# An encoder block on one core: at the projection's end, two form parts go to raw weight buffers, the last pair of rows is spread over the first units, and group 2's weight rows go behind it

## The chip, the cores and the metric

The kernel runs on one core of one Trainium2 chip. The metric is the device time of one execution in microseconds: before the change 1247.73 us, the median of three runs (1246.71 to 1248.21). Smaller is better.

## What is computed

One layer of a bidirectional encoder on 1024 tokens of width 1024, in float32:

```
u = RMSNorm(x);  [q|k|v|cB|cC|cH|gA|gB] = u @ W_in
y_A = neighbourhood_attention(q, k, v) @ W_A
y_B = (cB * conv3(cC * cH)) @ W_B
m = sigmoid(gA) * y_A + sigmoid(gB) * y_B
x = x + m @ W_o
x = x + relu(RMSNorm(x) @ W1)^2 @ W2
```

The change lies where `x + m @ W_o` (the projection, here) ends and `RMSNorm(x) @ W1` (the MLP's first product) begins.

## The kernel before

**Precision.** Every float32 operand is scaled and split into two float16 parts, a high and a low one; a product is three matmul passes (high x high, high x low, low x high). The high part is made by ACT, the low part by DVE.

**Seven products.** The MLP's first product is done by blocks with seven products instead of eight. The activations are therefore needed in seven *forms* (sums and differences of the four quarters of the rows; `sums` makes them with four additions), and the weights of each of 16 *groups* q in seven forms too. `U2[0]` (tile u2T) holds forms 0 to 3 of the activations, `U2[1]` (tile u2x) forms 4 to 6, each with high and low part and with 512 token positions.

**Pairs.** Rows are handled in four pairs: pair n holds blocks n and n + 4 of 128 tokens. For each pair `normal` scales the two blocks of x (ACT), `form_sums` makes the forms in one buffer (`fv[0]`, tile form; DVE), `high(n, part)` writes the high parts to a second buffer (`fv[1]`, tile v16; ACT, line 1193), and `low(n, part)` the low parts (DVE, line 1199), and then issues the transposing DMA (SP, line 1200) that puts the part in its place in `U2`. Part 0 is forms 0 to 3, part 1 forms 4 to 6. There is one form buffer and one v16 buffer, so a pair's high part waits for the transposes of the pair before.

**The order at the projection's end is written out by hand** (lines 1375 to 1404). `tail(b, half, ...)` issues one projection product of 24 matmuls (`proj`), and after it the listed operations. `sq` is a square with row sums (ACT), `row3` and `row_scale` the scale of a row (DVE, with one square root on ACT), `g1` one step of `forms_m`, which builds the seven weight forms of group 1 in spare places (one of them the tile `two` from the pool of raw weight buffers), and `tk` one step of the background list. The last pair, blocks 3 and 7, is a generator, `last_pair`, which is advanced by the units that follow.

**Units.** `unit` issues the matmuls of one product, then the evacuation of the product before (`late`), then so many `step`s of the foreground list `fg` and `tick`s of the background list `bg`. All engines work through their instructions in the order of issue. Groups 0 and 1 are each computed in two halves of 256 tokens, `quad(0, 0, 256)`, `quad(1, 0, 256)`, `quad(0, 256, 512)`, `quad(1, 256, 512)`, seven units each, with 3 steps and 5 ticks to a unit: these are the 28 half products of the text. The later groups run whole, seven units of 512 tokens. A product's result lies in one of eight PSUM banks, in three classes (d, s, o), taken in turn; it comes free with its evacuation: ACT's copy of product 1 (line 1457), DVE's `post6`, `post5`, `post2` (lines 1440, 1445, 1459), `post7` (lines 1448 to 1450), which frees three, and `post3` (1453).

**After a group.** `h_done(q)` squares the result on ACT (lines 1414, 1416), makes its seven forms with four additions on POOL (line 1159, called with `G`), and stores them to `hs` (line 1420). The result tile `as` has two buffers, so group q + 2 waits for the store of group q.

**The weights' chain** (background): `sums1(q)` scales the rows of the two raw parts (ACT, line 952), squares them for a bound (ACT, line 961) and adds forms (POOL, line 966); six half products later one column goes to a DVE cast (line 933), and two half products later a matmul with ones sums it over the partitions (`all_sum`, line 179). `prep1(q)` then takes the power of two from it (DVE, lines 182 to 412) and splits the forms (ACT line 981, DVE line 977), and goes on with `sums1(q + 1)`.

**Raw buffers.** The pool `rawp` has five buffers for raw weight parts of 512 KB. `load_upto` issues loads (SP, line 210) up to a count; `done` counts the parts that have been split, `held` the buffers lent to something else, `limit` the last part that may be loaded.

Of the kernel before, what the change touches and what calls it, by code (L numbers as in the profile page):

```python
# [10 lines left out]
F32 = mybir.dt.float32  # L11
F16 = mybir.dt.float16
BF16 = mybir.dt.bfloat16
I32 = mybir.dt.int32
AF = mybir.ActivationFunctionType
OP = mybir.AluOpType
# [36 lines left out]
def encoder_block(ctx: ExitStack, tc: tile.TileContext, x, weights, cols, gqk, rel, masks, out):  # L53
    nc = tc.nc
    V, A, G, T, SP = nc.vector, nc.scalar, nc.gpsimd, nc.tensor, nc.sync

    base = ctx.enter_context(tc.tile_pool(name="base", bufs=1))
    rawp = ctx.enter_context(tc.tile_pool(name="rawp", bufs=5))
# [38 lines left out]
    def at(c, i, n=1):  # L97
        return slice(c.start + i, c.start + i + n)
# [18 lines left out]
    fg, bg = [], []  # L117
# [88 lines left out]
    loads, loaded, done, vhome, held, limit = [], [0], [0], [], [0], [10 ** 6]  # L206
# [5 lines left out]
    def load_upto(n):  # L212
        while loaded[0] < min(n - held[0], limit[0], len(loads)):
            ch, p = loads[loaded[0]]
            loaded[0] += 1
            t = rawp.tile([128, 1024], F32, name="raw")
            load_into(t[:, :ch.widths[p][0] * ch.widths[p][1]], ch, p)
            ch.raw.append(t)
# [104 lines left out]
    g1, g2, gm2 = at(consts, 0, 8), at(consts, 20, 8), keep()  # L323
    rows = {"A": lambda j: rowsA, "B": lambda j: rowsB, "O": lambda j: rowsM}
    chunks, offset = {}, 0
    for (kind, j), pieces in plan():
# [4 lines left out]
        for p, (k, w) in enumerate(ch.widths):  # L331
            ch.offs.append(offset)
            if kind != "X" and (kind, j) != ("1", 0) and (kind, j, p) != ("1", 1, 1):
# [3 lines left out]
    cV, cConv, cA, cB, cO, c1, c2, c2x = ([chunks[k, j] for j in range(n)] for k, n in  # L337
                                              (("V", 2), ("C", 4), ("A", 4), ("B", 4), ("O", 2),
                                               ("1", 16), ("2", 4), ("X", 4)))
# [120 lines left out]
    sq = w1p.tile([128, D], F32, name="sq", bufs=1)  # L460
# [84 lines left out]
    for p in range(11):  # L545
# [7 lines left out]
        for q in (p,) if p < 6 else (2 * p - 6, 2 * p - 5):  # L553
            c = q // 2 + 3
# [306 lines left out]
    for k in range(N + 15):  # L861
        p, w = k // 16, k % 16
# [215 lines left out]
    for n in range(8):  # L1078
# [19 lines left out]
        else:  # L1098
            push(cO[0])
            tick(4)  # L1100
            y = w3p.tile([128, 4, 512], F32, name="gsum", bufs=1)
# [47 lines left out]
    U2 = (u2T,  # L1149
          w4p.tile([128, 3, 2, 4, 512], F16, name="u2x", bufs=1))  # L1150
# [4 lines left out]
    def sums(f, sub):  # L1155

        z = [f[:, i] for i in range(7)]
        for o, a, b, op in ((5, 0, 2, OP.subtract), (2, 2, 3, OP.subtract), (4, 2, 0, OP.subtract), (6, 1, 4, OP.add)):
            sub.tensor_tensor(z[o], z[a], z[b], op=op)  # L1159
            yield  # L1160

    pair_done, fv, ssq = [0], [], keep(10)
# [7 lines left out]
    def row_scale(col, n=1):  # L1170
        y = tmp(n)
        for _ in rstd(at(ssq, col, n), D, y, 9):
            pass
        return y

    def normal(b, y):
        A.activation(fv[0][:, 2 * (b // 4):2 * (b // 4) + 2].rearrange("p a t -> p (a t)"), X1[:, b], AF.Copy,
                     scale=sc[:, y])
# [9 lines left out]

    PART = ((0, 4), (4, 7))

    def high(n, part):
        a, b = PART[part]
        A.activation(fv[1][:, a:b, 0], fv[0][:, a:b], AF.Copy)

    def low(n, part):

        f, v = fv
        a, b = PART[part]
        V.tensor_tensor(v[:, a:b, 1], f[:, a:b], v[:, a:b, 0], op=OP.subtract)  # L1199
        SP.dma_start_transpose(U2[a // 4][:, :, :, :, 128 * n:128 * n + 128]  # L1200
                               .rearrange("p f s k t -> p (f s k) t"), v[:, a:b].rearrange("p f s k -> p (f s k)"))
        pair_done[0] = n + part

    def form_sums():
# [22 lines left out]
    def sums1(q):  # L1227

        ch = c1[q]
        if q == 2:  # L1230
            yield from rows_scaled(ch, g2)
        if q == 0:
            tsum[0] = U2[1][:, 2].rearrange("p s k t -> p (s k t)").bitcast(F32).rearrange("p (i c) -> p i c", i=4)
        elif q % 2 == 0:
            while q == 2 and pair_done[0] < 4:
                yield
            t = wsp.tile([128, 2, 4, 512], F32, name="tsum", tag="ws")
            for i in range(2):
                tsum[q + i] = t[:, i]
        if q != 2:  # L1240
            yield from rows_scaled(ch, g2)
        yield from forms_sum(ch, tsum[q], 3 if q else 0)

    def prep1(q):

        ch = c1[q]
        s, ch.inv = yield from scale_of(ch.sum, 9, 1)
        yield from gate(q)
        pool, tag = TAGS[q % 3]
        P = P1[q] = pool.tile([128, 7 if q else 8, 2, 512], F16, name="w16_1", tag=tag)  # L1250
        yield from forms_split(ch, tsum[q], s, P)
        ready.add(q)
        if 1 < q < 15:
            yield from sums1(q + 1)
# [1 line left out]
    SQJ = U2[1][:, 0, :, :, 384:512].rearrange("p s k t -> p (s k) t").bitcast(BF16)  # L1256
    scaled = []

    limit[0] = c1[3].first + 1

    def prep_m():

# [14 lines left out]
    def forms_m():  # L1277

        (w11, w12), (w21, w22) = ([c1[1].raw[i].rearrange("p (n m) -> p n m", n=2)[:, j] for j in range(2)]
                                  for i in range(2))  # L1280
        s = scaled[0]
        two = rawp.tile([128, 1024], F32, name="raw").bitcast(F16).rearrange("p (f i c) -> p f i c", f=2, i=2)
        held[0], limit[0] = 1, 10 ** 6
        t2 = w4p.tile([128, 2, 512], F16, name="t2", bufs=1)
        t4 = w4p.tile([128, 2, 512], F16, name="t4", bufs=1)
        k4 = lambda v: v.rearrange("p (k c) -> p k c", k=4)
        flat = {0: lambda i: P1[0][:, 7, i], 1: lambda i: two[:, 0, i], 2: lambda i: two[:, 1, i],
                5: lambda i: t2[:, i], 6: lambda i: t4[:, i]}

        def place(f, i):  # L1290
            return k4(flat[f](i)) if f in flat else M[0][:, 4 * (f - 3):4 * (f - 3) + 4, 512 * i:512 * i + 128]

        P1[1] = lambda f, i, k: place(f, i)[:, k]
        src = {0: w11, 1: w21, 2: w22, 3: w11, 4: w12, 5: w22, 6: w21}

        def hi(f):
            A.activation(place(f, 0), k4(src[f]), AF.Copy, scale=sc[:, s])

        def lo(f):
            V.scalar_tensor_tensor(place(f, 1), k4(src[f]), sc[:, s], place(f, 0), op0=OP.mult, op1=OP.subtract)  # L1300

        def add(o, a, b):
            V.tensor_tensor(o, a, b, op=OP.add)

        hi(0), hi(2), hi(1), lo(0), add(w11, w11, w12), lo(2)
        yield
        add(w12, w12, w22)
        yield
        add(w22, w22, w11), lo(1), hi(5), add(w21, w21, w22), hi(6)
        yield  # L1310
        lo(5), lo(6)
        yield
        hi(3), hi(4), lo(3)
        yield
        lo(4)
        done[0] += 1
        load_upto(done[0] + 5)
        ready.add(1)

# [15 lines left out]
    def wait(n):  # L1335
        for _ in range(n):
            yield
# [7 lines left out]
    two = []  # L1345
# [9 lines left out]
    def tail(b, half, *acts):  # L1355
        proj(b, half, acts)
        for a in acts:
            a()
# [3 lines left out]
    def sq(b, half=None):  # L1362
        if half is None:
            return lambda: square(b, 2 * (b % 4) + b // 4)
        return lambda: square(b, (6 if half == 0 else 8) + b // 4, slice(512 * half, 512 * half + 512))

    def row3(b):
        V.tensor_tensor(sc[:, at(ssq, 6 + b // 4)], sc[:, at(ssq, 6 + b // 4)], sc[:, at(ssq, 8 + b // 4)], op=OP.add)
        return row_scale(6 + b // 4)

    def do(f, *a):
        return lambda: f(*a)

    g1, tk = do(advance, chain), do(tick)
# [6 lines left out]
    tail(5, 1, sq(1), form_sums, do(high, 0, 0), g1)  # L1381
    tail(2, 1, do(high, 0, 1), sq(5), do(low, 0, 0), do(begin, 1), do(low, 0, 1))
    tail(6, 1, sq(2), form_sums, do(high, 1, 0))
    tail(3, 0, sq(6), do(high, 1, 1), do(low, 1, 0), do(begin, 2), do(low, 1, 1))
    tail(7, 0, sq(3, 0), form_sums, do(high, 2, 0), g1)
    bg.append(sums1(2))
    tail(3, 1, sq(7, 0), do(low, 2, 0), do(high, 2, 1), do(low, 2, 1), g1, tk)
    side[0] = False
    bg.extend(prep1(q) for q in range(2, 16))
    tail(7, 1, sq(3, 1), lambda: normal(3, row3(3)), tk)  # L1390
    fv[1] = wsp.tile([128, 7, 2, 512], F16, name="v16", tag="ws")

    def last_pair():
        sq(7, 1)()
        y = row3(7)
        yield from wait(3)
        normal(7, y)
        yield from wait(6)
        form_sums()
        high(3, 0), high(3, 1)  # L1400
        yield from wait(6)
        low(3, 0), low(3, 1)

    fg.append(last_pair())
    pe_done[0] = 0
# [6 lines left out]
    def h_done(q):  # L1412
        f = AS.pop(q)
        A.activation(f[:, 0:4], f[:, 0:4], AF.Relu)  # L1414
        yield
        A.activation(f[:, 0:4], f[:, 0:4], AF.Square, scale=sc[:, c1[q].inv],  # L1416
                     accum_out=sc[:, at(bsum[q // 4], q % 4)])
        yield
        yield from sums(f, G)
        SP.dma_start(HS[q // 4][:, :, q % 4], f)  # L1420
        live.remove(q)
        if q % 4 == 3:
            m = tmp()
            V.tensor_reduce(sc[:, m], sc[:, bsum[q // 4]], axis=AX, op=OP.max)
            yield
            yield from pow2(m, 14, *R[q // 4])
            r_ready[q // 4] = True
# [293 lines left out]
```

## Time and profile before

| | |
|---|---|
| Median of three runs | 1247.73 us |
| The profiled execution's own time | 1246.2 us |
| Its span, first to last instruction | 1244.4 us |
| Mean granted TensorE clock | 0.995 |
| PE busy | 1199.2 us, 96% |
| DVE busy | 926.9 us, 74% |
| ACT busy | 765.3 us, 61% |
| POOL busy | 437.0 us, 35% |

PE is TensorE's matmuls, DVE is VectorE, ACT ScalarE, POOL GpSimd, and SP the queue that issues DMAs. Times in the views are microseconds from the first instruction. A line of a timeline is: start, length, engine, line of the kernel, operation, out<-in by tile names, shape, count of merged instructions, and in brackets how long the engine stood idle before it and what ended that. A line of the waits is: who waited <- for whom, total, times, longest. A line of the windows gives for each stretch the busy time of PE, PE's weight loads, DVE, ACT and POOL, each with its count of instructions, then the granted clock of PE, the share and the rate of the DMAs. A line of the DMA issues ends with the time from issue to landing. The projection ends and the MLP begins at 646 us.

### The profile page before, as it was taken

The page shows a single profiled execution, that of the slowest core. Times are in us where ns is not written, and L with a number is a line of the kernel's source. Part 1 is how long each engine was busy: PE and PEld are TensorE (multiplying, and loading weights), DVE is VectorE, ACT ScalarE, POOL GpSimd, SP SyncE. Part 2 cuts the span into 40 slices and gives each one's busy share as a digit, 9 for nine tenths or more (in the row PEclk, how much of TensorE's full clock was granted, in tenths as well). Part 3 has the DMA queues.
Part 4 walks back from the last instruction along what each step waited for, and adds up shares of the span by engine and source line. Part 5 has one row for each costly group of instructions (what it writes and reads, how often), then busy time and mean ns, then how long its engine had stood idle before and what let it go on. Part 6 is the DMA issues. An engine that isn't in the chain of part 4 may idle for free. (4 is left out here: it accounts for less than half of the span.)

```text
span 1244.4 us, 17059 instructions
## 1 busy us (share of the span) xinstructions
PE 1199.2 (96%) x6294; PEld 575.2 (46%) x6294; DVE 926.9 (74%) x1733; ACT 765.3 (61%) x1177; POOL 437.0 (35%) x297
## 2 busy tenths in 40 slices
PE   4989999999999999999997899999999999999998
PEld 3534444444444444444456444444444444444444
DVE  6668777988557686887877655554546989999997
ACT  5777577787464454536666877877865763645430
POOL 2440003111331111101002756556557463373562
PEclk8999999999999999999998999999999999999999
DMA  6458456665651211216185454543575754436202
GB/s 256 105 191 179 82 121 135 136 120 114 135 144 40 68 51 51 68 35 253 55 164 122 157 177 149 186 151 134 182 273 175 273 192 139 170 111 241 102 34 102
DMA packets 170803, 173.35 MB, mean 139 GB/s; under 512 B 131424, under 2 KB 131936, under 8 KB 166624
## 3 DMA queue, kind: packets, MB, share of 16 engines
q1 hardware_dynamic: 170720, 172.27, 47.4%
q8 instruction: 49, 0.80, 0.3%
q14 instruction: 34, 0.28, 0.1%
HBM read 102.51 MB, written 37.75 MB: 113 GB/s over the span
## 5 line engine op out<-in xcount | busy, mean ns | idle before, releaser
L188 PEld LDWEIGHTS <-ops 128*128 128x128 f16 x1356 | 132.4, 98 | 159.4 <-issue 2.6
L188 PEld LDWEIGHTS <-w 128*128 128x128 f16 x1368 | 132.8, 98 | 142.9 <-issue 3.6
L859 PE MATMUL ps_d<-uT,w_ws 128*128 128x512 f16 x528 | 125.4, 379 | 0.0
L188 PE MATMUL ps_d<-ops 128*128 128x512 f16 (+1 forms) x528 | 118.3, 374 | 0.0
L188 PE MATMUL ps_s<-ops 128*128 128x512 f16 x492 | 113.2, 379 | 1.5 <-DVE ops L1554 1.1
L1545 ACT ACTIVATE ops<-hf,sc 128x2048 f16<-128x2048 f32 x26 | 52.0, 1999 | 95.5 <-PE ps_o L188 34.8
L1159 POOL TENSOR_TENSOR as<-as 128x512 f32<-128x512 f32 x64 | 88.0, 1376 | 40.6 <-ACT as L1416 36.9
L188 PEld LDWEIGHTS <-uT 128*128 128x128 f16 x648 | 64.5, 100 | 70.1 <-issue 5.3
L966 POOL TENSOR_TENSOR tsum<-raw 128x512 f32<-128x512 f32 x28 | 46.2, 1666 | 137.1 <-ACT raw L952 137.1
L188 PEld LDWEIGHTS <-w_s 128*128 128x128 f16 x588 | 56.8, 98 | 69.4 <-DVE w_s L977 1.9
L188 PE MATMUL ps_d<-u2x,w 128*128 128x512 f16 (+1 forms) x360 | 80.0, 372 | 0.0
L1547 DVE SCALAR_TENSOR_TENSOR ops<-hf,sc,ops 128x2048 f16<-128x2048 f32 x26 | 74.1, 2849 | 5.2 <-ACT ops L1545 5.2
L188 PE MATMUL ps_o<-ops 128*128 128x512 f16 x336 | 77.1, 379 | 0.0
L859 PEld LDWEIGHTS <-w_ws 128*128 128x128 f16 x528 | 50.8, 98 | 52.5
L188 PE MATMUL ps_o<-u2T,w 128*128 128x512 f16 (+1 forms) x324 | 71.7, 371 | 0.0
L952 ACT ACTIVATE raw<-raw,sc 128x256 f32<-128x256 f32 x172 | 70.9, 493 | 0.0
L966 POOL TENSOR_TENSOR gsum<-raw 128x512 f32<-128x512 f32 x14 | 19.0, 1376 | 131.6 <-issue 57.1
L981 ACT ACTIVATE w<-raw,sc 128x512 f16<-128x512 f32 (+1 forms) x28 | 24.6, 927 | 52.9 <-DVE sc L411 52.9
L1440 DVE TENSOR_TENSOR as<-ps_d,as 128x512 f32<-128x512 f32 (+1 forms) x15 | 10.1, 674 | 63.1 <-ACT as L1457 63.1
L806 ACT ACTIVATE sz<-sz,sc 128x384 f32<-128x384 f32 (+1 forms) x64 | 37.3, 582 | 26.5 <-DVE sc L810 13.2
L188 PE MATMUL ps_s<-u2T,w 128*128 128x512 f16 (+1 forms) x252 | 52.7, 359 | 0.0
L278 DVE SCALAR_TENSOR_TENSOR w_ws<-raw,sc,w_ws 128x512 f16<-128x512 f32 (+2 forms) x72 | 46.1, 691 | 2.4 <-ACT w_ws L291 2.4
(333 smaller groups left out, 2611.6 us busy)
## 6 DMA issues: line engine op xcount, KB each, us to landing
raw<-in_weights SPq DMA_DIRECT2D x89, 512.0 KB, 5.3
hs<-as SPq DMA_DIRECT2D x16, 1792.0 KB, 8.7
hf<-hs SPq DMA_DIRECT2D x26, 1024.0 KB, 6.3
w2x<-in_weights SPq DMA_DIRECT2D x16, 512.0 KB, 8.3
raw<-in_weights SPq DMA_DIRECT2D x16, 384.0 KB, 4.0
xt<-in_x SPq DMA_DIRECT2D x8, 512.0 KB, 10.0
gs<-s SPq DMA_DIRECT2D x4, 1024.0 KB, 6.8
x<-in_x SPq DMA_DIRECT2D x8, 512.0 KB, 9.9
```

The source lines that it names most:

```text
L188: T.matmul(ps, l, r, start=a, stop=b)
L278: V.scalar_tensor_tensor(lo, self.raw[p][:, o:o + m], sc[:, c:c + 1], hi, op0=OP.mult, op1=OP.subtract)
L806: A.activation(z, z, AF.Exp, scale=-1.0, bias=sc[:, d["mx"]], accum_out=sc[:, d["sm"]])
L859: T.matmul(ps, l, r, start=a, stop=b)
L952: A.activation(v, v, AF.Copy, scale=sc[:, at(g, 4 * i + k)])
L966: G.tensor_tensor(t[:, o], a, b, op=OP.add)
L981: A.activation(o(0), w, AF.Copy, scale=sc[:, s])
L1159: sub.tensor_tensor(z[o], z[a], z[b], op=op)
L1440: V.tensor_tensor(z[5], ps[6], z[4], op=OP.add)
L1545: A.activation(P[:, 1, 0], hf, AF.Copy, scale=sc[:, Rs])
L1547: V.scalar_tensor_tensor(P[:, 1, 1], hf, sc[:, Rs], P[:, 1, 0], op0=OP.mult, op1=OP.subtract)
```

## The change

Three things are done.

1. **Raw buffers as form buffers.** `forms_m` takes three raw buffers instead of one. Two of them (`spare`) hold the high and low parts of pair 1's part 0 and pair 2's part 1, each as pieces of at most two forms; each piece has its own ACT and DVE instruction and its own transposing DMA. Because the buffers are lent out, only one part of group 2's raw weights is loaded before; the other follows at the end of `forms_m`, and group 3's two parts at the end of `last_pair`.
2. **The last pair is spread out.** `normal(7)` is issued at once, the form sums and high parts three steps later, `low(3, 0)` six steps later, then, after three steps, the background list gets the weights' chain of group 2 (`sums1(2)`, before this in the tails) and of all later groups, and six steps later follow `low(3, 1)` and the loads. `sums1(2)` no longer waits for the last pair. In the tails the order changes too: `low(1, 0)` and the row scale come ahead of `high(1, 1)`, the steps of `forms_m` go one tail later and in one part more.
3. **The forms of groups 0 and 1** are added on DVE instead of POOL.

```diff
+    spare = []
+    def pieces(n, part):
+        a, b = PART[part]
+        if (n, part) not in ((1, 0), (2, 1)):
+            return [(a, b, fv[1][:, a:b])]
+        return [(c, min(c + 2, b), spare[i][:, :min(2, b - c)]) for i, c in enumerate(range(a, b, 2))]
     def high(n, part):
-        a, b = PART[part]
-        A.activation(fv[1][:, a:b, 0], fv[0][:, a:b], AF.Copy)
+        for a, b, v in pieces(n, part):
+            A.activation(v[:, :, 0], fv[0][:, a:b], AF.Copy)
     def low(n, part):
-        f, v = fv
-        a, b = PART[part]
-        V.tensor_tensor(v[:, a:b, 1], f[:, a:b], v[:, a:b, 0], op=OP.subtract)
-        SP.dma_start_transpose(U2[a // 4][:, :, :, :, 128 * n:128 * n + 128]
-                               .rearrange("p f s k t -> p (f s k) t"), v[:, a:b].rearrange("p f s k -> p (f s k)"))
+        for a, b, v in pieces(n, part):
+            V.tensor_tensor(v[:, :, 1], fv[0][:, a:b], v[:, :, 0], op=OP.subtract)
+            SP.dma_start_transpose(U2[a // 4][:, a % 4:a % 4 + b - a, :, :, 128 * n:128 * n + 128]
+                                   .rearrange("p f s k t -> p (f s k) t"), v.rearrange("p f s k -> p (f s k)"))
...
         elif q % 2 == 0:
-            while q == 2 and pair_done[0] < 4:
-                yield
...
-    limit[0] = c1[3].first + 1
+    limit[0] = c1[2].first
...
-        two = rawp.tile([128, 1024], F32, name="raw").bitcast(F16).rearrange("p (f i c) -> p f i c", f=2, i=2)
-        held[0], limit[0] = 1, 10 ** 6
+        three = [rawp.tile([128, 1024], F32, name="raw").bitcast(F16).rearrange("p (f i c) -> p f i c", f=2, i=2)
+                 for _ in range(3)]
+        spare.extend(three[:2])
+        two = three[2]
+        held[0], limit[0] = 3, c1[2].first + 1
+        load_upto(done[0] + 5)
...
-        hi(3), hi(4), lo(3)
+        hi(3), hi(4)
+        yield
+        lo(3)
         yield
         lo(4)
         done[0] += 1
+        held[0], limit[0] = 1, c1[3].first
         load_upto(done[0] + 5)
...
-    tail(3, 0, sq(6), do(high, 1, 1), do(low, 1, 0), do(begin, 2), do(low, 1, 1))
-    tail(7, 0, sq(3, 0), form_sums, do(high, 2, 0), g1)
-    bg.append(sums1(2))
-    tail(3, 1, sq(7, 0), do(low, 2, 0), do(high, 2, 1), do(low, 2, 1), g1, tk)
+    y = []
+    tail(3, 0, sq(6), do(low, 1, 0), lambda: y.append(row_scale(4, 2)), do(high, 1, 1),
+         lambda: (normal(2, at(y[0], 0)), normal(6, at(y[0], 1))), do(low, 1, 1))
+    tail(7, 0, sq(3, 0), form_sums, do(high, 2, 0), do(high, 2, 1))
+    tail(3, 1, sq(7, 0), do(low, 2, 0), g1, do(low, 2, 1))
     side[0] = False
-    bg.extend(prep1(q) for q in range(2, 16))
-    tail(7, 1, sq(3, 1), lambda: normal(3, row3(3)), tk)
+    tail(7, 1, sq(3, 1), g1, lambda: normal(3, row3(3)), g1)
...
         sq(7, 1)()
-        y = row3(7)
+        normal(7, row3(7))
         yield from wait(3)
-        normal(7, y)
-        yield from wait(6)
         form_sums()
         high(3, 0), high(3, 1)
         yield from wait(6)
-        low(3, 0), low(3, 1)
+        low(3, 0)
+        yield from wait(3)
+        bg.append(sums1(2))
+        bg.extend(prep1(q) for q in range(2, 16))
+        yield from wait(6)
+        low(3, 1)
+        limit[0] = 10 ** 6
+        load_upto(done[0] + 5)
...
-        yield from sums(f, G)
+        yield from sums(f, G if q > 1 else V)
```

## The prediction

> **What bounds the kernel now.** I read the waits of PE first, over the projection's end and the first half of the MLP (600 to 760 us), because PE is the engine that hardly rests, and only a wait of PE can be saved. There are two:
>
> ```profile
> PE ps_s L188 <- DVE as L1448: 6.3, 1, 6.3
> PE ps_s L179 <- DVE ones L933: 3.3, 1, 3.3
> ```
>
> Next the timeline of PE shows where they lie and what they cost.
>
> ```profile
> 646.12 1.47 PE L188 MATMUL ps_s<-u2T,w 128*128 128x256 f16 x12
> 647.43 1.47 PE L188 MATMUL ps_d<-u2x,w 128*128 128x256 f16 x12
> ...
> 665.67 2.71 PE L188 MATMUL ps_s<-u2T,t 128*128 128x256 f16 x12 [6.29 <-DVE as L1448]
> ...
> 668.18 1.64 PE L188 MATMUL ps_o<-u2T,raw 128*128 128x256 f16 x12
> ...
> 669.66 1.47 PE L188 MATMUL ps_d<-u2x,mH 128*128 128x256 f16 x12
> ...
> 704.49 0.16 PE L179 MATMUL ps_s<-ones 128*128 128x1 bf16 x1 [3.29 <-DVE ones L933]
> ```
>
> Groups 0 and 1 are computed as 28 half products of 12 matmuls, the first at 646.12, one each 1.31 us (647.43 - 646.12); a whole product of the later groups takes twice that. Half product 11 waits 6.29 us. After it two half products start 2.51 and 1.48 us apart instead of 1.31, which is 1.37 us more. The windows of 1 us say why (the number before the DMA share is the granted clock):
>
> ```profile
> 661.00:662.00 1.00, 0.00 (x0) 0.00 (x0) 0.75 (x2) 1.00 (x2) 0.00 (x0) 0.85 0.00 0
> ...
> 668.00:669.00 1.00, 1.00 (x8) 0.81 (x7) 0.00 (x0) 0.00 (x0) 0.00 (x0) 0.74 1.16 217
> ...
> 702.00:703.00 1.00, 0.00 (x0) 0.00 (x0) 0.00 (x0) 0.82 (x3) 0.24 (x1) 1.00 1.04 373
> ```
>
> The clock fell at 661.7, some 2.3 us after PE stopped, and came back at 668.5; the second wait of 3.29 us left it at 1.00. So the first wait costs 6.29 + 1.37 = 7.66 us, the second 3.29: 10.95 us are to be had, no more.
>
> The first wait's reason is on DVE, which has the last pair's work ahead of L1448, the operation that frees a bank:
>
> ```profile
> 651.23 0.74 DVE L1328 SCALAR_TENSOR_TENSOR x<-ps_d,sc,x 128x512 f32<-128x512 f32 x1
> ...
> 655.49 0.15 DVE L391 TENSOR_SCALAR sc<-sc 128x1 f32<-128x1 f32 x1
> ...
> 657.87 2.87 DVE L1159 TENSOR_TENSOR form<-form 128x512 f32<-128x512 f32 x4 [0.24 <-ACT form L1177]
> ...
> 661.33 3.96 DVE L1199 TENSOR_TENSOR v<-form,v 128x2048 f16<-128x2048 f32 x2 [0.25 <-ACT v L1193]
> 665.20 0.42 DVE L1448 TENSOR_TENSOR as<-ps_s,as 128x256 f32<-128x256 f32 x1
> ```
>
> The second wait is for group 4's all-sum (L933), which stands on DVE behind L1440, and that behind ACT's copy, which needs the store of group 0 landed, issued 8.9 us earlier. But ACT had been idle for only 0.18 us by then, so the store isn't the only late one.
>
> ```profile
> 693.89 0.61 SPq L1420 DMA_DIRECT2D hs<-as  x1
> ...
> 702.86 0.60 ACT L1457 ACTIVATE as<-ps_o 128x512 f32<-128x512 f32 x1 [0.18 <-DMA hs<-as]
> ...
> 704.28 0.16 DVE L933 CAST ones<-sc 128x1 bf16<-128x1 f32 x1
> ```
>
> **First part of the change: the last pair spread out.** normal(7) is now issued in half product 1, the form sums in 2, the first low part in 4, the second in 7, behind the bank-freeing operations of group 0 (post7) instead of ahead of them. These ACT rows complete the chain:
>
> ```profile
> 654.00 0.61 ACT L1167 ACTIVATE u2x<-x 128x512 bf16<-128x512 f32 x1
> ...
> 656.69 1.15 ACT L1177 ACTIVATE form<-x,sc 128x1024 f32<-128x1024 f32 x1 [0.54 <-DVE sc L400]
> ...
> 659.38 3.28 ACT L1193 ACTIVATE v<-form 128x2048 f16<-128x2048 f32 x2 [1.54 <-DVE form L1159]
> ```
>
> The last projection result is there at about 646.3. DVE adds it (0.74), ACT squares (0.8 with the accumulator), DVE adds the two half sums (0.2), scale to normal is 1.2 (655.49 to 656.69), normal 1.15: 650.4. Form sums 2.87: 653.3; high(3,0), 1.85, can begin at the third sum: 654.5; low(3,0), 2.2: 656.8; one bank operation, 0.4, then L1448, done by 657.6. Half product 11 wants it at 646.12 + 10 x 1.31 = 659.2. It has 1.6 us to spare, so the wait goes, and with it the slow clock: -7.66. From both sides: 0 spare if every link of this chain were 15% longer; a gain beyond 7.66 isn't possible there.
>
> What is late next?
>
> ```profile
> u2T<-v SPq DMA_TRANSPOSE x1, 6.9
> ...
> u2T<-v SPq DMA_TRANSPOSE x1, 8.5
> ```
>
> low(3,0)'s transposes go out at 656.8. Those of pairs 0 and 1 landed in 6.9 us, the last pair's in 8.5, so here 663.7 to 665.3, for half product 15 at 664.5: at worst a wait of 0.8 us, which a later wait would swallow. low(3,1) runs 658.1 to 659.9 on DVE, its transposes 661.5, and half product 19 (669.7) is the first to read them.
>
> **Second part: raw buffers.** high(1,0) no longer waits for the transposes of pair 0, at the price of smaller instructions.
>
> ```profile
> 620.54 4.72 SPq L1200 DMA_TRANSPOSE u2T<-v  x1
> ...
> 625.36 3.76 SPq L1200 DMA_TRANSPOSE u2x<-v  x1
> ```
>
> Four forms hold SP's queue for 4.72 us, three for 3.76: 0.96 a form and 0.9 for each issue. Two parts become four, so SP gets two issues more, 1.8 us; ACT and DVE get two instructions more each, about 0.2 us apiece. PE's 10 projection products cover that, and the first halves of groups 0 and 1 read only pairs 0 and 1, issued by 635 and landed within 7 us. I count nothing; without that cover it would be 2 us. The buffers are paid for by weights: the second part of group 2's rows is now loaded behind the transposes of pair 2, and both parts of group 3's behind those of pair 3.
>
> ```profile
> 649.84 3.98 SPq L1200 DMA_TRANSPOSE u2x<-v  x1
> 653.92 0.53 SPq L210 DMA_DIRECT2D raw<-in_weights  x1
> ```
> ```profile
> raw<-in_weights SPq DMA_DIRECT2D x1, 512.0 KB, 3.9
> ...
> hs<-as SPq DMA_DIRECT2D x1, 1792.0 KB, 8.9
> raw<-in_weights SPq DMA_DIRECT2D x2, 512.0 KB, 9.6
> ```
>
> 3.9 us is the landing of the load at 653.92, which also went out right behind a transpose; 9.6 that of two loads right behind the store of group 0. Nothing but the transposes is ahead here, so I take 3.9: group 2's part goes out at 650.5, lands at 654.4, and ACT reaches it at 657.5. Group 3's go out at 665.3 and land at 669.2 and 670.5 or so, while ACT comes to them at 669.3. There is nothing to spare: at 9.6 everything behind moves by 5.4 us.
>
> **Third part: the weights' chain and the sums.** Group 2's four adds are issued in half product 5 (before: 6), so its all-sum matmul stands behind half product 13 (before: 14), at 646.12 + 13 x 1.31 = 663.15. Before, DVE's first operation on its result came at 672.82 (below). From there ACT is the longest queue:
>
> ```profile
> 674.10 1.75 ACT L981 ACTIVATE w<-raw,sc 128x512 f16<-128x512 f32 x2
> ...
> 677.83 3.29 ACT L952 ACTIVATE raw<-raw,sc 128x256 f32<-128x256 f32 x8
> 681.03 1.04 ACT L961 ACTIVATE tsum<-raw 128x1024 f32<-128x1024 f32 x1
> ...
> 683.25 1.89 ACT L1414 ACTIVATE as<-as 128x2048 f32<-128x2048 f32 x1
> 685.18 2.00 ACT L1416 ACTIVATE as<-as,sc 128x2048 f32<-128x2048 f32 x1
> ```
>
> Split 3.73, rows scaled 3.20, squares 2.22, relu and square 4.02 (start to start, the last to 687.27): 13.2 us a group. DVE's six small operations between all-sum and split take 0.95:
>
> ```profile
> 672.82 0.15 DVE L182 TENSOR_SCALAR sc<-ps_o 128x1 f32<-128x1 f32 x1
> ...
> 673.64 0.14 DVE L412 TENSOR_SCALAR sc<-sc 128x1 int32<-128x1 int32 x1
> ```
>
> The sums of groups 0 and 1 go from POOL to DVE:
>
> ```profile
> 687.35 6.52 POOL L1159 TENSOR_TENSOR as<-as 128x512 f32<-128x512 f32 x4 [1.23 <-ACT as L1416]
> ```
>
> On DVE four take 2.87 (L1159 above) instead of 6.52, and group 0's store leaves 3.65 us sooner after the square. But DVE's order is fixed: behind these sums stand group 1's bank operations and the scale of group 3's weights, and for group 1 two of the sums and L1440 stand ahead of L933 of group 4.
>
> Laid end to end: post7 of group 1 and the six operations end at 665.2; ACT 3.73 and one copy 0.36: 669.3, group 3's rows landed; 3.20 + 2.22 + 4.02 : 678.8; DVE sums 2.87, a bank operation 0.34, six operations 0.95: 683.0; ACT 13.2: 696.2; DVE two sums 1.4, L1440 0.7, a third sum 0.7, L932 and L933 0.4: 699.4. Before it was 704.44, so group 4's all-sum comes **5.1 us sooner**, not 10.95. Two of these steps are bounded from both sides: sums at 6.5 like POOL's instead of 2.87 would add 3.6 and 2; a DVE that waits for nobody would take off 1. POOL's adds of group 4 lie at 689 to 695, between DVE's splits (684 to 689) and its sums, so I charge no slowing of one by the other.
>
> PE runs ahead of that: 28 half products end at 682.8. The third product of group 2 wants a bank that group 1's post7 frees; that stands behind group 3's split on DVE and comes at about 689.8, against 688.0: a wait of 1.8. The fourth ends at 695.0, and PE waits to 699.4: 4.4 us. This second wait is longer than the one before, and longer than the one that left the clock alone. The clock fell after 2.3 idle us at 661.7, so I expect it to fall again, and charge the same 1.37; the ends are 0 (as at 702) and 3.4 (half of a slow stretch of 6.8 us, all of it busy).
>
> In the Trainium skill, "TensorE: Matmul & The Clock Gate", section "What's actually happening", the clock falls after a whole idle window of about 3.4 us on a grid that runs freely. By that rule a wait of 4.4 us falls surely on a whole window in only about 3 of 10 positions, and the sum would be 5.1 without the 1.37. The 2.3 us of the trace speak against taking it literally.
>
> **Sum.** -5.1 + 1.4 = -3.7 us.
>
> ```profile
> PE ps_s L188 <- DVE ops L1554: 1.1, 2, 0.8
> ```
>
> This is the largest wait of PE behind 704, two of at most 0.8 us, and group 2's later work stands to PE as before, so I count nothing given back. The profiled execution, 1246.2 us with a span of 1244.4, would become 1242.5 (span 1240.7). The median of the runs before lies 1.5 us above it, 1247.73, so I forecast **1244.0**.
>
> **Rivals.**
> - *The clock stays full* in the new wait: -5.1, 1242.6. For it: 3.29 us left it alone. Chance 0.16.
> - *Both waits close*, PE then runs through: -10.95, 1236.8. It needs ACT's two rounds of 13.2 us to shrink by 6; only shorter DVE work speaks for it. 0.06.
> - *Taken back*: ACT's chain loses 2 to 4 us more (sums beside POOL, a late transpose), so that the all-sum comes at 701.5 to 704 and the clock falls too: -1.6 to +1, about 1247.5. 0.21.
> - *Slower*: the loads of group 3 land as the 9.6 row says. ACT, in order, stands before the row scaling until 674.9; L933 of group 3 follows at 674.9 + 3.2 + 2.2 + 0.5 = 680.8, where PE, behind half product 24, stands from 677.6; group 4's all-sum comes at 699.4 + 5.5 = 704.9, and two or three of the waits bring the clock down, 1.4 each: 704.9 + 2.8 to 4.2 against 704.4, so +3.3 to +4.7, about 1251.7. It costs more than the change gains from a landing of some 7.5 us on. 0.13.
> - *Forecast*: 0.44, from 1241.5 to 1246.
>
> About 0.2% (2.5 us) is what a measurement here can tell from no change. Faster: nearly all of the forecast, and the first two, 0.64; same: the third and a little of the forecast, 0.23; slower 0.13. The range reaches from 1240.5 (leaving out the full gain) to 1248.5 (leaving out the slow case).
>
> **What would show it.** Right: L1448 has gone from PE's waits; half product 28 ends near 683; a wait of 1 to 3 us for L1449 in group 2's third product; L933's wait has grown to 4 or 5 us, ending near 699.5; a stretch at half clock there and none at 661; the store of group 0 issued near 682. Wrong: group 3's loads landing over 5 us, a wait for L933 behind half product 24, or L1159 on DVE well over 0.7 us each.

## The result, and the profile after

| | before | after |
|---|---|---|
| Median | 1247.97 us (4 runs, 1246.71 to 1248.92) | 1241.83 us (4 runs, 1240.83 to 1242.68) |
| Profiled execution, its span | 1246.2, 1244.4 us | 1241.45, 1239.7 us |
| First half product to group 4's all-sum | 58.37 us | 53.67 us |
| All-sum to the end of the span | 539.9 us | 540.3 us |

The ratio is 0.9951, with a 95% interval of 0.9934 to 0.9968: faster by 0.5%, some 6 us by the medians and 4.75 us between the two profiled executions. In the changed file the lines stand lower: 1202 high parts, 1207 low parts, 1466 to 1468 the three operations of `post7` (before 1448 to 1450), 1458 and 1475 the first evacuations (1440, 1457), 1438 the store to `hs` (1420), 1434 the square (1416).

The waits of PE from 600 to 760 us, after:

```profile
PE ps_s L188 <- DVE as L1467: 2.4, 1, 2.4
PE ps_s L179 <- DVE ones L933: 2.0, 1, 2.0
```

The 6.3 us are gone and the wait for L933 is shorter, but a new one has come. The timeline of PE, after, shows where:

```profile
645.75 1.47 PE L188 MATMUL ps_s<-u2T,w 128*128 128x256 f16 x12
...
658.85 1.47 PE L188 MATMUL ps_s<-u2T,t 128*128 128x256 f16 x12
...
662.78 0.17 PE L179 MATMUL ps_s<-ones 128*128 128x1 bf16 x1
...
682.69 2.75 PE L188 MATMUL ps_o<-u2T,w 128*128 128x512 f16 x12
...
690.39 4.23 PE L188 MATMUL ps_s<-u2T,w 128*128 128x512 f16 x12 [2.36 <-DVE as L1467]
694.41 3.00 PE L188 MATMUL ps_d<-u2T,w 128*128 128x512 f16 x12
699.42 0.16 PE L179 MATMUL ps_s<-ones 128*128 128x1 bf16 x1 [2.01 <-DVE ones L933]
699.45 2.75 PE L188 MATMUL ps_o<-u2T,w 128*128 128x512 f16 x12
```

Half product 11 starts at 658.85 without a wait, and the 28 half products run through to 682.69. Group 2's third product waits 2.36 us for a bank and then takes 4.23 us instead of 2.75: the clock has fallen (its windows are shown further down). Group 4's all-sum comes at 699.42 (704.49 before), and behind it the clock is full. What stands behind the all-sum runs as before. DVE and ACT, after:

```profile
645.95 0.75 DVE L1341 SCALAR_TENSOR_TENSOR x<-ps_d,sc,x 128x512 f32<-128x512 f32 x1 [0.59 <-PE ps_d L188]
...
650.13 2.87 DVE L1159 TENSOR_TENSOR form<-form 128x512 f32<-128x512 f32 x4 [1.22 <-ACT form L1177]
...
653.78 2.28 DVE L1207 TENSOR_TENSOR v<-form,v 128x2048 f16<-128x2048 f32 x1
...
656.31 0.41 DVE L1466 TENSOR_TENSOR as<-ps_s,as 128x256 f32<-128x256 f32 x1
```
```profile
669.87 3.30 ACT L952 ACTIVATE raw<-raw,sc 128x256 f32<-128x256 f32 x8 [0.71 <-DMA raw<-in_weights]
...
677.22 2.00 ACT L1434 ACTIVATE as<-as,sc 128x2048 f32<-128x2048 f32 x1
```

The form sums that began at 657.87 now begin at 650.13; `post7`, at 665.20 before, stands at 656.31. Group 3's loads cost ACT 0.71 us, and nothing else in this stretch waits for a load.

### The profile page after: what moved, and what is told of

Read it like the earlier page. It is cut to its first block, busy times and chain, and to the rows that moved or that the text cites. A ratio compares the mean times of both kernels' runs of the same rounds, so it can differ in the third digit from the quotient of the medians.

```text
span 1239.7 us, 17066 instructions
## 1 busy us (share of the span) xinstructions
PE 1200.9 (97%) x6294; PEld 575.6 (46%) x6294; DVE 930.0 (75%) x1743; ACT 765.2 (62%) x1179; POOL 425.5 (34%) x289
## 4 chain that ended last, share of the span: by engine, by line
PE 67%; DVE 18%; ACT 7%; issue 4%; DMA 1%; POOL 1%; SPq 0%; DVEq 0%; ACTq 0%; POOLq 0%
PE ps_d L188 26%; PE ps_s L188 20%; PE ps_o L188 18%; PE ps_d L859 3%; DVE sz L797 2%; DVE P L823 2%; DVE w_s L977 2%; DVE w_ws L278 1%; DVE ops L1572 1%; POOL sform L481 1%; DMA raw<-in_weights 1%; ACT w_ws L241 1%; ACT as L1432 1%; DVE sc L302 1%; DVE sg L1093 1%
## 5 line engine op out<-in xcount | busy, mean ns | idle before, releaser
L1159 POOL TENSOR_TENSOR as<-as 128x512 f32<-128x512 f32 x56 | 76.6, 1369 | 37.1 <-ACT as L1434 33.8
```

## The experiments

My theory after the result: the spread of the last pair takes the first wait away, the buffers are the means to load and place things, the sums on DVE shorten the chain to group 4's all-sum. The rival was that one of the three parts does nearly all. "To all-sum" is the time from the first half product to group 4's all-sum in the profiled execution, "behind" from there to the end of the span. Each kernel was compared with runs of before on its chip, whose median was 1247.9 to 1248.0 us, and 1246.7 for the last four kernels.

| kernel | median us | ratio to before (95%) | to all-sum | behind |
|---|---|---|---|---|
| before | 1247.97 | | 58.37 | 539.9 |
| after | 1241.83 | 0.9951 (0.9934 to 0.9968) | 53.67 | 540.3 |
| e1 sums of all groups on POOL | 1240.10 | 0.9939 (0.9918 to 0.9959) | 52.07 | 540.1 |
| e2 no raw buffers | 1245.87 | 0.9983 (0.9972 to 0.9994) | 57.60 | 541.8 |
| e3 last pair at its old places | 1242.82 | 0.9963 (0.9948 to 0.9978) | 54.35 | 541.6 |
| e4 both | 1248.69 | 1.0007 (0.9997 to 1.0018) | 59.01 | 541.9 |
| e5 before, sums on DVE | 1251.70 | 1.0030 (1.0020 to 1.0040) | 61.19 | 541.5 |
| e6 before once more, one run | 1246.89 | | 58.28 | 540.7 |
| e7 all-sum one product later | 1292.79 | 1.0351 (1.0328 to 1.0374) | | |
| e8 the same, sums on POOL, loads early | 1288.97 | 1.0324 (1.0307 to 1.0341) | | |
| e9 after, sums on POOL, loads early | 1238.52 | 0.9927 (0.9914 to 0.9939) | 50.46 | 540.1 |
| e10 after, group 1's sums on POOL | 1241.19 | 0.9949 (0.9935 to 0.9962) | 52.04 | 540.0 |
| e11 buffers for pair 1's part alone | 1243.10 | 0.9965 (0.9952 to 0.9978) | 53.79 | 541.9 |
| e12 buffers for pair 2's part alone | 1244.41 | 0.9973 (0.9962 to 0.9985) | 56.15 | 540.2 |

**e2, no raw buffers.**

```diff
     def pieces(n, part):
-        if (n, part) not in ((1, 0), (2, 1)):
-            return [(a, b, fv[1][:, a:b])]
-        return [(c, min(c + 2, b), ...) for ...]
+        return [(a, b, fv[1][:, a:b])]
```

> The changed kernel with all form parts in the one v16 buffer (the raw buffers stay lent out, unused, and the loads stay as they are). My theory: the raw buffers carry the first wait's removal together with the order of the tails; without them the tails run some 3 us later on ACT and DVE, a wait of 0.5 to 1.5 us for post7 comes back at half product 11, group 2's all-sum is 1 to 2 us late, and the time rises by 2 to 3 us. The rival (the spreading of the last pair is what removes the wait, and the buffers are worth nothing): no wait at half product 11, the time within 0.5 us of the changed kernel.

Measured: 1245.87 us, 4.0 above after. The profile shows the reason ahead of the half products. The timeline of ACT, first after, then e2, at the high parts:

```profile
624.29 1.99 ACT L1202 ACTIVATE raw<-form 128x1024 f16<-128x1024 f32 x2
...
635.85 1.91 ACT L1202 ACTIVATE v<-form 128x2048 f16<-128x2048 f32 x1 [0.59 <-ACT u2x L1167]
637.67 1.56 ACT L1202 ACTIVATE raw<-form 128x1024 f16<-128x1024 f32 x2
```
```profile
627.04 1.91 ACT L1200 ACTIVATE v<-form 128x2048 f16<-128x2048 f32 x1 [2.34 <-DVE x L1339]
...
638.32 1.91 ACT L1200 ACTIVATE v<-form 128x2048 f16<-128x2048 f32 x1 [2.09 <-DMA u2T<-v]
641.86 1.48 ACT L1200 ACTIVATE v<-form 128x1536 f16<-128x1536 f32 x1 [1.63 <-DMA u2x<-v]
```

In e2 pair 2's last high part comes 4.2 us later (641.86 against 637.67), because v16 must first be read out by the transposes of pair 1. Group 2's all-sum, with all of its chain, then waits too. The timeline of PE, e2:

```profile
664.54 0.16 PE L179 MATMUL ps_s<-ones 128*128 128x1 bf16 x1 [1.03 <-DVE ones L933]
...
694.17 4.44 PE L188 MATMUL ps_s<-u2T,w 128*128 128x512 f16 x12 [3.96 <-DVE as L1465]
703.20 0.16 PE L179 MATMUL ps_s<-ones 128*128 128x1 bf16 x1 [2.01 <-DVE ones L933]
```

So the buffers carry most of the gain of this kernel, though PE never waits for a transpose in the projection.

**e11 and e12, one of the two buffers each.**

```diff
-        if (n, part) not in ((1, 0), (2, 1)):
+        if (n, part) != (1, 0):        # e11;  e12: (2, 1)
```

> After with raw buffers for the second pair's first part alone; the third pair's last part goes through v16 as before, and waits there for the transposes of the second pair's last part. Theory (the second pair's part carries the gain: it starts 2.8 us sooner and everything behind it follows; the third pair's last part loses some 3 us on ACT, of which DVE's low part hides most): 1241.6 to 1243.0 us. Rival (the third pair's part carries it, since it is the last before the final pair): 1244 to 1246 us.

> After with raw buffers for the third pair's last part alone. Theory (without the second pair's buffers the third pair's first part still waits for its transposes, 2.1 us, as with no raw buffers at all): 1244.3 to 1245.9 us. Rival (the third pair's part carries the gain): 1241.8 to 1243.2 us.

Measured: 1243.10 and 1244.41 us, the first 0.1 us above what was expected, the second within it, on a chip where before ran 1.3 us lower. e12 has the expected wait for the transposes ahead of pair 2's first part (2.12 us on ACT) and loses 2.5 us up to the all-sum. e11 loses next to nothing there (53.79 us against 53.67); its profiled execution is longer behind the all-sum, by 1.7 us, because its clock falls there. The timeline of PE, e11:

```profile
691.53 2.75 PE L188 MATMUL ps_s<-u2T,w 128*128 128x512 f16 x12 [2.40 <-DVE as L1467]
...
700.57 0.16 PE L179 MATMUL ps_s<-ones 128*128 128x1 bf16 x1 [3.69 <-DVE ones L933]
```

After loses the clock in the bank wait (2.36 us) and keeps it in the second (2.01); e11 keeps it in a bank wait of 2.40 us and loses it in the second, 3.69. That the missing buffer does this isn't shown: e3, below, has both buffers and the same two waits (2.45 and 3.69 us), and behind them the same fall. The medians, with intervals of some 1.6 us to each side, don't separate e11 from after; by the time to the all-sum, pair 1's buffer is the larger part.

**e3 and e4, the last pair at its old places,** with and without the buffers.

```diff
-        normal(7, row3(7))
+        y = row3(7)
         yield from wait(3)
+        normal(7, y)
+        yield from wait(6)
         form_sums()
         high(3, 0), high(3, 1)
-        yield from wait(6)
-        low(3, 0)
         yield from wait(3)
         bg.append(sums1(2))
         bg.extend(prep1(q) for q in range(2, 16))
-        yield from wait(6)
-        low(3, 1)
+        yield from wait(3)
+        low(3, 0), low(3, 1)
```

> The changed kernel with the last pair's steps at their old places (normal in half product 2, form sums in 4, both low parts in 6, so ahead of post7 again); raw buffers, tails and sums stay as changed. My theory: with the tails early, DVE has the low parts done by 658 all the same, post7 follows at 658.5, just in time for half product 11 at 658.9: wait of 0 to 0.5 us, and the time within 0.5 us of the changed kernel. The rival (the place of the low parts behind post7 removes the wait): the wait for L1448's successor comes back with 3 to 6 us, and the time rises by 3 us or more.

> Both together: no raw buffers and the last pair at its old places. My theory: the parts cover for one another; with both gone the first wait comes back with 3 to 4.5 us (and the half clock with it), the all-sum of group 4 at about 704, the time 4 to 5.5 us above the changed kernel, and little of the gain is left. The rival: the same rise as with the last pair alone.

Measured: e3 1242.82, e4 1248.69 us. The timelines of DVE, first e3, then e4:

```profile
651.07 2.87 DVE L1159 TENSOR_TENSOR form<-form 128x512 f32<-128x512 f32 x4
...
654.53 3.96 DVE L1207 TENSOR_TENSOR v<-form,v 128x2048 f16<-128x2048 f32 x2 [0.25 <-ACT v L1202]
658.41 0.42 DVE L1466 TENSOR_TENSOR as<-ps_s,as 128x256 f32<-128x256 f32 x1
```
```profile
655.10 2.87 DVE L1159 TENSOR_TENSOR form<-form 128x512 f32<-128x512 f32 x4
...
662.43 0.42 DVE L1464 TENSOR_TENSOR as<-ps_s,as 128x256 f32<-128x256 f32 x1
```

In e3 the whole low part, 3.96 us, stands ahead of `post7` as before, and still `post7` comes at 658.41, in time for half product 11: the wait does not return. With neither part it comes at 662.43, PE waits 3.78 us, and the gain is gone. So the buffers close the first wait without the spread; the spread without the buffers nearly does it too (e2: a wait of 0.55 us there), but e2's later waits (3.96 and 2.01 us) remain. All of these runs keep the new order of the tails. e4 differs from e5 below only in that order, in the place of group 2's chain and in the loads, and lies 3.0 us lower by the medians; no run undoes these alone, so their share of the gain is open.

**e1, the sums of groups 0 and 1 back on POOL,** in the changed kernel; **e5, the sums on DVE** in the kernel before; **e10, group 0's on DVE, group 1's on POOL.**

```diff
-        yield from sums(f, G if q > 1 else V)
+        yield from sums(f, G)                     # e1
+        yield from sums(f, G if q else V)         # e10
```
```diff
-        yield from sums(f, G)
+        yield from sums(f, G if q > 1 else V)     # e5, in before
```

> The changed kernel with the forms of groups 0 and 1 added on POOL again. My theory: the sums on DVE hurt here, since behind them DVE holds the scale of group 3's weights; on POOL that scale comes about 2.5 us sooner and the two sums ahead of group 4's all-sum go too, so the all-sum comes at 696 to 697 instead of 699.4, and the time falls by 2.5 to 3.5 us against the changed kernel. The rival (the sums on DVE are what brings the store of group 0 and so the second wait forward): the store leaves at 685 to 686 instead of 682.5, the wait ends 2 to 3 us later, the time rises by as much.

> The kernel before with one part of the change alone: the forms of groups 0 and 1 added on DVE. My theory: the first wait stays 6.3 us; the sums hold up the scale of group 3's weights and stand ahead of group 4's all-sum, whose wait of 3.3 us stays or grows, and a new wait for group 3's all-sum or a bank appears; group 4's all-sum comes 1 to 3 us later than before, the time rises by 1 to 3 us. The rival (DVE's sums bring the store forward and so shorten the second wait): the time falls by 2 to 3 us.

> After with group 0's sums on DVE as in the change and group 1's on POOL as before. Theory (group 1's sums stand on DVE just ahead of group 4's all-sum, so theirs is the cost; group 0's stand where DVE had waited): all-sum 4 about 1.5 us sooner, at 697.5 to 698.3, the bank wait as in after (2.4 us): 1239.6 to 1240.4 us. Rival (group 0's sums are the cost, by delaying group 3's scale): no gain, 1241.4 to 1242.2 us.

Measured: 1240.10, 1251.70 and 1241.19 us. The change of the sums by itself is a loss: 3.7 us on the kernel before by the medians, although the first wait of e5 is 4.88 us and not 6.3 as expected. The edit lies behind that wait; what differs most ahead of it is one operation of DVE, first before, then e5:

```profile
646.66 1.78 DVE L1300 SCALAR_TENSOR_TENSOR mH<-raw,sc,mH 128x512 f16<-128x512 f32 x1
```
```profile
645.69 0.75 DVE L1300 SCALAR_TENSOR_TENSOR mH<-raw,sc,mH 128x512 f16<-128x512 f32 x1
```

In before, and in e6, POOL's first add for group 2's chain starts 0.03 to 0.04 us ahead of L1300, and DVE takes 1.03 us longer; in e5 it starts 0.21 us behind, and POOL takes longer (1.66 us for 1.26). In the changed kernel this add comes 10 us later, so some 1 us of the first wait lies with that meeting, as far as three profiles show it, and went with the new place of the chain; the other 0.4 us of the difference are not traced.
 On the changed kernel the trace of e1 has the all-sum 1.6 us sooner (52.07 against 53.67); the medians say 1.7, within their intervals. Why it isn't more, the timelines show. DVE in e1, and POOL beside it:

```profile
682.85 3.12 DVE L977 SCALAR_TENSOR_TENSOR w<-raw,sc,w 128x512 f16<-128x512 f32 x2 [0.73 <-ACT w L981]
685.90 4.50 DVE L977 SCALAR_TENSOR_TENSOR w<-tsum,sc,w 128x1024 f16<-128x1024 f32 x2
...
691.56 0.42 DVE L1467 TENSOR_TENSOR as<-ps_s,as 128x256 f32<-128x256 f32 x1
...
698.02 0.16 DVE L933 CAST ones<-sc 128x1 bf16<-128x1 f32 x1
```
```profile
680.59 6.52 POOL L1159 TENSOR_TENSOR as<-as 128x512 f32<-128x512 f32 x4 [1.24 <-ACT as L1434]
```

And the same stretch of DVE, after:

```profile
679.35 1.42 DVE L1159 TENSOR_TENSOR as<-as 128x512 f32<-128x512 f32 x2 [3.58 <-ACT as L1434]
...
681.02 1.41 DVE L1159 TENSOR_TENSOR as<-as 128x512 f32<-128x512 f32 x2
...
686.28 2.47 DVE L977 SCALAR_TENSOR_TENSOR w<-tsum,sc,w 128x1024 f16<-128x1024 f32 x2
...
696.50 1.42 DVE L1159 TENSOR_TENSOR as<-as 128x512 f32<-128x512 f32 x2 [5.50 <-ACT as L1434]
```

Group 0's sums on DVE push group 3's scale back by 2.4 us (from the square's end to L182 3.0 us after, 0.6 in e1); on POOL they slow DVE's split of group 3 by about as much, 7.5 us from first to last instead of 4.7 (4.50 against 2.47 for the same two instructions). Group 1's sums on DVE stand straight ahead of L933. That is the cost: from the square's end to L933 it takes 2.7 us after (696.47 to 699.21) and 1.3 in e1 (696.72 to 698.02). e10 takes the better half of each, and its profiled execution has the shortest second wait of all (0.6 us) and an all-sum 1.6 us sooner; but its runs lie in two clusters, at 1239.6 to 1240.5 and 1241.9 to 1242.1, so that its median shows no gain. Its profiled execution belongs to the first; what the others met isn't shown.

**e7, group 4's all-sum one product later.**

```diff
-        yield from forms_sum(ch, tsum[q], 3 if q else 0)
+        yield from forms_sum(ch, tsum[q], 4 if q == 4 else 3 if q else 0)
```

> The changed kernel with group 4's all-sum issued one product of group 2 later (its gap counted as 4 instead of 3), nothing else. My theory: PE's wait for L933 is only a matter of where the small matmul stands in PE's order; one product later L933 is there first, and the wait of 2.0 us goes, while the bank wait of 2.4 us stays: the time falls by 1.5 to 2 us. The rival (PE would then wait for the same chain somewhere else, a bank or group 4's weights): the wait moves to the next products, the time within 0.5 us.

Measured: 1292.79 us, 51 us more, a plain miss. The waits of PE from 700 to 1000 us in e7:

```profile
PE ps_o L179 <- DVE ones L933: 28.0, 9, 4.1
PE ps_o L179 <- DVE sc L108: 10.8, 3, 3.9
```

The shift is handed on: group 5's rows are taken up when group 4 is split, so every later group's all-sum moved too. ACT then had the two operations of group 2's square (L1432 and L1434) among the scaling of group 5's rows instead of behind it, and stood idle for 5.81 us ahead of the first, until DVE's L1471 was done. The timeline of ACT, first after, then e7:

```profile
705.17 3.29 ACT L952 ACTIVATE raw<-raw,sc 128x256 f32<-128x256 f32 x8
...
714.51 0.58 ACT L1475 ACTIVATE as<-ps_o 128x512 f32<-128x512 f32 x1
```
```profile
711.78 1.91 ACT L1432 ACTIVATE as<-as 128x2048 f32<-128x2048 f32 x1 [5.81 <-DVE as L1471]
713.60 1.69 ACT L952 ACTIVATE raw<-raw,sc 128x256 f32<-128x256 f32 x4
...
721.00 0.58 ACT L1475 ACTIVATE as<-ps_o 128x512 f32<-128x512 f32 x1
```

The copy of the first product comes 6.5 us later, L933 stands behind its evacuation on DVE, and PE waits again in each group: 38.8 us of waits, and a clock of 0.94 in the windows from 780 to 960. A slot in the order isn't a delay of one operation; it is the phase of a cycle that all later groups repeat.

**e8, the same with the sums on POOL and group 3's loads issued in half product 1; e9, the same without the shift.**

```diff
         normal(7, row3(7))
         yield from wait(3)
+        limit[0] = 10 ** 6
+        load_upto(done[0] + 5)
...
         low(3, 1)
-        limit[0] = 10 ** 6
-        load_upto(done[0] + 5)
```

> The changed kernel with the sums on POOL, group 4's all-sum one product later, and group 3's raw loads issued at half product 1, ahead of the last pair's transposes. My theory: the bank wait of 2.4 us goes with the sums, the all-sum's wait with its place, the 0.7 us that ACT waits for the load with its earlier issue; PE then runs through from the projection to the second product, some 4.5 us below the changed kernel, about 1237. The rival: POOL's sums slow DVE's splitting so far that the bank wait stays at 2 us or more, and only 2 to 3 us are won.

> After with the sums of all groups on POOL and group 3's two loads issued in half product 1, ahead of the last pair's transposes. Theory (what DVE and ACT have to do sets the all-sum of group 4, the loads are hidden but for the 0.71 us that ACT waited for them at 669.87): 0 to 0.8 us off the kernel with the sums on POOL alone (1240.1), so 1239.3 to 1240.2 us. Rival (the loads share the DMA queues with the last pair's transposes, which then land later): PE waits for transposes in half product 15 or 19, 1241 to 1243 us.

Measured: 1288.97 us for e8, with the cause of e7, and **1238.52 us for e9**, the fastest of all, at a ratio of 0.9927, and some 0.8 us lower than expected, where before ran 1.3 us lower as well. e9 holds e1's edit too, e8 also e7's. The load that ACT waited for 1.50 us in e1 (0.71 after) is there, and PE, e9, has two short waits left:

```profile
690.56 2.75 PE L188 MATMUL ps_s<-u2T,w 128*128 128x512 f16 x12 [1.95 <-DVE as L1467]
...
696.75 0.16 PE L179 MATMUL ps_s<-ones 128*128 128x1 bf16 x1 [0.85 <-DVE ones L933]
```

No transpose is waited for; the rival, that the loads would delay them, falls.

**e6, the kernel before once more,** for the clock in its waits.

> The kernel before, unchanged, for a second profile. The medians of before and after lie 6.1 us apart, the two profiled executions 4.75. My theory: the clock's grid starts elsewhere in each execution, so the second wait of 3.3 us meets the clock gate in some executions and not in others; if it does here, a stretch at half clock follows it and the execution takes about 1.4 us more than the first profile's 1246.2. The rival: the clock is as in the first profile, half only around 662 to 668, and the difference is of another kind.

Measured: 1246.89 us, a first wait of 6.3 us with the half clock from 662.2 us on, a second of 3.0 with the clock full. So this run has the clock of the first profile, and the theory of a second stretch isn't shown.

## Why the prediction was right, and where it wasn't

**The direction, the all-sum and the order of events were right.** Forecast and measured: `post7`'s first operation done by 657.6 (656.7); the end of the half products 682.8 (682.7); group 2's all-sum 663.15 (662.78); its load out at 650.5 (649.67); group 3's loads out at 665.3 (665.25), with ACT at 669.3 (669.87); group 0's store near 682 (682.50); group 4's all-sum **699.4 (699.42)**. The bank wait was put at 1.8 us and is 2.36. That the all-sum agrees to 0.02 us is in part luck: the first half product began 0.37 us sooner than before, and its start lies anywhere from 645.4 to 646.8 us in the runs. Counted from there the all-sum comes 4.70 us sooner, not 5.1.

**The step that failed in size: "I expect it to fall again, and charge the same 1.37"** behind a second wait of 4.4 us. The clock fell one wait earlier, in the bank wait. Products three and four of group 2 took 7.0 us (690.39 to 697.41) instead of the 5.3 of the first two, but PE would have waited for 699.4 anyway, so the slow stretch cost nothing; it only shortened the second wait to 2.01 us, after which the clock stayed full. The term was 0 in this execution where 1.37 was charged; another 0.3 us behind the all-sum was not forecast, and the two profiles of before (539.9 and 540.7) differ by more. That makes the profiled execution 1241.45 instead of 1242.5, near the 1241.1 of the rival with the full clock, but not by its mechanism: the clock did fall, one wait sooner, where it was free. The windows, after, at the edges of the slow stretch:

```profile
688.08:691.49 3.41, 1.10 (x6) 0.51 (x6) 2.85 (x7) 3.38 (x9) 2.37 (x2) 1.00 0.99 292
691.49:694.90 3.41, 3.41 (x10) 1.17 (x9) 0.00 (x0) 3.38 (x4) 2.32 (x3) 0.50 0.23 90
```

The term itself exists: where the clock falls behind the all-sum (e2, e3, e4, e5, e11) the rest of the span takes 541.5 to 541.9 us, and 539.9 to 540.7 in the others of the table, 1.6 us less by the means. In e3 and e11 it came just where the forecast had it, behind a second wait of 3.69 us. Which of the two waits takes the clock is the luck of one execution: by the windows of the last section, an estimate, the bank wait of 2.36 us takes it in about half of the positions of the grid, and the second wait in the others.

**"The median of the runs before lies 1.5 us above" its profiled execution, carried over to the changed kernel, was wrong:** the changed kernel's median lies only 0.4 above its own. That is the other 1.1 us of 2.2. The runs of before spread from 1244.4 to 1250.8 us, at granted clocks from 0.990 to 0.996; those of after from 1240.8 to 1242.7. The second wait of before, 3 us at the edge of losing the clock, could add one stretch of 3.41 us. It can't be all: against the profiled execution at 0.995, a run at 0.990 has some 12 us more at half clock (an estimate, 0.005 of 1244 us for half the speed). No trace of a long run of before shows where, so the cause stays open.

**What the sum hid.** "I count nothing" for the buffers was wrong as an account, though not in the total. The first step had the last pair's chain begin at 646.3, when PE has its result. Before, DVE came to it only at 651.23, behind pair 2's low parts (642.69 to 646.75), which had waited for v16, and the work queued after them. Counted from the first half product, DVE comes to it after 5.1 us in before, 0.2 in after, 0.3 in e3, 3.0 in e2 and 2.8 in e4. So that DVE would be free at 646 was the gift of the buffers (2.6 to 2.8 us) and, for the rest, of the new order with group 2's chain taken out of the tails (2.1 to 2.3 us), and the forecast booked it to the spread of the last pair. e2 shows what the buffers are worth in the whole, 4 us.

**The sums on DVE** were booked as a saving (2.87 us for 6.52). Each sum takes 0.72 us, as forecast, but group 1's lie ahead of L933, and the change loses 1.6 us by the sums (e1, by the profiled executions). The remark that DVE's order is fixed had named the place. The alternative was priced with the wrong sign: "sums at 6.5 like POOL's instead of 2.87 would add 3.6 and 2". That lays POOL's time on the chain, where it doesn't lie, since on POOL neither the scale of group 3's weights nor L933 stands behind the sums; and "I charge no slowing of one by the other" left out what POOL's sums do cost, 2.8 us in DVE's split.

The rival that was slower by late loads did not come: they were issued behind transposes as forecast, and cost ACT 0.71 us instead of 5.4. Nor did both waits close: 4.4 us of waiting are left (2.4 and 2.0).

## What to carry to other kernels

Before a gain is booked to a new order, ask which buffer let the engine reach that point at all, and undo the parts one by one: two parts may each close the same wait. A faster engine for a step gains nothing if its queue holds what the chain ends on; here the slower engine, off the chain, was ahead by 1.6 us in the profiled executions. Move a step of a repeating chain only with the whole cycle in view, since a shift of one product was paid in every later group.

## What the runs showed of the hardware

**The clock falls by windows, not by the length of a wait.** Within one execution the slow stretches begin at distances that are whole multiples of 3.413 us (e2: 694.26 and 704.50; e5: 64.92, 662.26 and 706.63, which is 175 and 13 steps) and last 3.41 or 6.83 us. Laid on this grid, which lies differently in each execution, the 14 profiles agree: from 600 to 1225 us, each window at full clock in which PE was idle for 0.59 or more of it was followed by a window at half clock, and none of those up to 0.58. Windows of e1, which waited 3.39 us and kept its clock, and of e10, which waited 2.05 us and lost it:

```profile
687.18:690.59 3.41, 1.47 (x7) 0.59 (x6) 3.41 (x3) 3.38 (x8) 2.98 (x2) 1.00 0.65 244
690.59:694.00 3.41, 1.96 (x10) 0.89 (x10) 1.99 (x6) 2.08 (x3) 3.33 (x3) 1.00 1.02 291
```
```profile
686.97:690.38 3.41, 1.36 (x7) 0.57 (x6) 3.34 (x8) 3.41 (x9) 1.57 (x2) 1.00 1.01 274
690.38:693.79 3.41, 3.41 (x10) 1.23 (x9) 0.31 (x1) 3.38 (x5) 2.32 (x3) 0.50 0.48 180
```

The number behind the length is PE's busy time: 1.47 and 1.96 of 3.41 us in e1, a wait split over two windows; 1.36 in e10, enough in one. In the Trainium skill, "TensorE: Matmul & The Clock Gate", section "What's actually happening", the window is 3413 ns and runs freely, which these runs bear out; that it needs an idle window they bear out only as one idle for about 59%. Worked out from the runs' 0.59 of 3.41 us, a single wait under 2.0 us can't lose the clock here and one over 4.0 us must; between them it is the place of the grid that decides.

**DVE and POOL beside each other.** L977 on two 128x1024 tiles takes 2.47 us alone and 4.50 while POOL adds; POOL's four sums take 6.52 us beside it and 5.32 later in after (714.68), where DVE is mostly idle. The Trainium skill, "GPSIMD Engine Reference", section "1. Specifications", says that POOL shares its SBUF interfaces with VectorE, with contention where DVE's instruction has two SBUF inputs. The trace agrees: L977 has two.
